# 1/rms of fourteen norms moved from ScalarE's square root to a bit-level seed and three Newton steps on VectorE

## The chip, the cores and the metric

The program runs on one core of a Trainium2 chip. A core has five engines with a queue each: TensorE (PE; its weight loads are shown apart as PEld), VectorE (DVE), ScalarE (ACT), GpSimd (POOL) and SyncE (SP, which here issues nearly all DMAs). Every engine works its own queue in order, and engines wait for each other through semaphores. The metric is the time of one execution in microseconds of the device; lower is better.

## The reference, cut to what matters

One inference step of a decoder trunk with two layers: 512 prompt tokens and 32 sample tokens (8 sequences of 4) of width 1024. Layer 0 mixes tokens with gated linear attention (GLA), layer 1 with sliding-window attention; both also attend to a memory of 256 tokens. Each layer is a SwiGLU network, the token mix, and a second SwiGLU network, and each of the three starts with an RMS norm. There is one more norm ahead of the shared keys and values, one at the end, one over each head of the GLA output, and one over the memory tokens.

```python
def rmsnorm(x, g):
    xf = x.astype(jnp.float32)
    y = xf * lax.rsqrt(jnp.mean(xf * xf, axis=-1, keepdims=True) + EPS)
    return (y * g.astype(jnp.float32)).astype(x.dtype)

def swiglu_half(x, g, w_gu, w_down):
    h = rmsnorm(x, g)
    gate, up = jnp.split(h @ w_gu, 2, axis=-1)
    return 0.5 * ((jax.nn.silu(gate) * up) @ w_down)
```

In each of two layers: `x += swiglu_half(x)`, `x += [tokmix(rmsnorm(x)); memattn(rmsnorm(x))] @ w_out`, `x += swiglu_half(x)`. All inputs and outputs are float32.

## The kernel before, in words

The tokens lie transposed, 128 features to a tile and eight tiles to the width, in two halves: h0 is 256 prompt tokens and the 32 sample tokens (288 columns), h1 the other 256 prompt tokens. Every product of float32 numbers is made of three products of shorter numbers: each operand is split into a rounded part (on ScalarE, L298) and the remainder (on VectorE, L299). So each tile of weights (128x1024, names ending in r as loaded, h and l as split) costs ScalarE about 1.06 us and VectorE about 1.23 us before TensorE can use it, and each tile of activations has such a pair too. A dense product (L356) is 24 matmuls into one PSUM bank: eight feature tiles by three. Three banks (bank_67, bank_68, bank_69 in the order below) take turns for these products, so a product waits until the values of the one three before have been read out of its bank.

The second half of the width of the hidden layer runs as a Strassen-like pair product of both halves (L342), for which `pair` forms sums and differences on VectorE.

A norm is `rstd` (L394): TensorE adds the squares over the features with a column of ones (L404), VectorE scales the mean and adds EPS (L410, two or three columns of 128 numbers), `rsqrt` (L424) makes 1/rms, VectorE multiplies the identity matrix with it (L414), TensorE spreads the diagonal over all partitions with a matrix of ones (L416), and ScalarE copies that out of PSUM (L421). Then `normed` multiplies the tokens (L438) and splits them (L298, L299). `rsqrt` also serves the norm over the GLA heads (L860, twelve columns, named ov).

ScalarE evaluates its functions from tables that hold one set of functions at a time. [...] Where the next function is not in the present set, an instruction ACT_TABLE_LOAD stands ahead of it in ScalarE's queue and bears the line of that function.

Names of norms used below, in order of time: mix_0 is the norm ahead of layer 0's token mix, for h0 at 355 us and for h1 at 543 us; the one for keys and values of h0 at 1066 us; mix_1 for h0 at 1478 us and for h1 at 1630 us; the norms ahead of the two pair products of the second networks at 802 and 1799 us; the final norm of h1 at 2138 us, after which nothing is left but the output. Around mix_0 h0, the keys' norm and mix_1 h0 the same piece of code runs: the norm of h0 is made while TensorE multiplies the last third of the first network for h1 (products g0, u0, g1, u1, g2, u2: gate and up; `late` or `first` in `layer` and `run`).

The order of the instructions within an engine's queue is not that of the code. It is chosen when the kernel is built, by a scheduler that places each instruction by priorities (`high_priority`) and by its own estimate of when it could start, and that also chooses which free weight buffer a load goes to. So a changed instruction list can move others that the code does not touch.

Of the kernel before, what the change touches and what calls it, by code (L numbers as in the profile page):

```python
# [11 lines left out]
F32 = mybir.dt.float32  # L12
F32R = mybir.dt.float32r
U8 = mybir.dt.uint8
AF = mybir.ActivationFunctionType
ALU = mybir.AluOpType
AX = mybir.AxisListType
# [215 lines left out]
class Build:  # L233
# [61 lines left out]
    def split_into(self, h, l, src, scale=None):  # L295
        nc = self.nc
        if scale is None:
            nc.scalar.activation(h, src, AF.Copy)  # L298
            nc.vector.tensor_tensor(out=l, in0=src, in1=h.bitcast(F32), op=ALU.subtract)  # L299
        else:  # L300
            nc.scalar.activation(h, src, AF.Copy, scale=scale)
            nc.vector.scalar_tensor_tensor(out=l, in0=src, scalar=scale, in1=h.bitcast(F32),
# [57 lines left out]
    def copy(self, out, ps, scale=1.0):  # L360
        with self.tc.high_priority(offset=self.AHEAD):
            self.nc.scalar.activation(out, ps, AF.Copy, scale=scale)
        return out
# [6 lines left out]
    def stats(self, x, h):  # L370
# [3 lines left out]
        if self.seen[h] in (1, KD):  # L374
            sq = self.u(n)
            nc.scalar.activation(sq, x, AF.Square)
            self.acc[h].append(sq)
        else:
            sq = self.sqs.u(n)
            nc.scalar.activation(sq, x, AF.Square)  # L380
            nc.vector.tensor_tensor(out=self.acc[h][0], in0=self.acc[h][0], in1=sq, op=ALU.add)
# [12 lines left out]
    def rstd(self, h, banks=None, keep=True):  # L394
# [25 lines left out]
        r = self.u(n)  # L420
        nc.scalar.activation(r, pr[:, :n], AF.Copy)  # L421
        return r

    def rsqrt(self, v, s, t):  # L424
        nc = self.nc
        nc.scalar.activation(s, v, AF.Sqrt)
        nc.vector.reciprocal(t, s)
        nc.vector.scalar_tensor_tensor(out=s, in0=t, scalar=-0.5, in1=t, op0=ALU.mult, op1=ALU.mult)
        nc.vector.tensor_tensor(out=s, in0=s, in1=v, op=ALU.mult)
        nc.vector.scalar_tensor_tensor(out=t, in0=s, scalar=1.5, in1=t, op0=ALU.add, op1=ALU.mult)  # L430

    def normed(self, h, norm, r):
        nc = self.nc
# [919 lines left out]
    def run(self):  # L1353
        nc, d = self.nc, self.d
# [6 lines left out]
        self.mr = None  # L1361
        self.vt, self.state = [None] * 5, [None] * GH
        self.x = [[], []]
        self.layer_ = 0
        with self.tc.high_priority(offset=self.FIRST):
            self.gains = self.const("gains")
            nc.scalar.activation(self.small("set", 1), self.one, AF.Sqrt)
# [31 lines left out]
        nc.vector.tensor_scalar(out=self.gout, in0=self.gout, scalar1=0.5, scalar2=None, op0=ALU.mult)  # L1399
        self.masks = self.cp.tile([P, 9, P], U8, tag="masks", name="masks")  # L1400
        for j in range(3):
            t = self.ld("mask", [P, 3, P])
# [7 lines left out]
        for o, i in (("o_kc", "ckr"), ("o_vc", "cvr")):  # L1410
            nc.sync.dma_start(d[o], d[i][:, 4 * 192:])

        rest = self.layer(0, self.in_a, self.attend_a, d["a_out"], xs)
        r = self.rstd(0)
        xk = self.normed(0, "kv", r)
# [90 lines left out]
```

## Time and profile before

| what | value |
|---|---|
| three timed runs | 2155.02, 2154.74, 2149.47 us; median 2154.74 |
| the profiled execution | 2148.32 us, of which 2146.5 us from the first to the last instruction |
| TensorE busy | 2065.4 us, 96% of the span |
| VectorE busy | 1539.5 us, 72%, 3234 instructions |
| ScalarE busy | 1067.2 us, 50%, 2089 instructions |
| mean granted clock of TensorE | 0.983 of full speed |

The busy shares are means over stages with different limits; what a change in one place is worth is read from who waits there. The time outside the span (1.8 us) is the same kind of start and end for every execution. The granted clock is 1 at 2.4 GHz and 0.5 at 1.2 GHz.

### The profile page before, as it was taken

The numbers are of one execution on the slowest core, as the hardware profiler recorded it, in microseconds if no ns is written. First come the engines' busy times: TensorE is split into PE (matmuls) and PEld (weight loads), VectorE is DVE, ScalarE is ACT, GpSimd is POOL, SyncE is SP. The second block draws the span as 40 slices with busy tenths as digits, with TensorE's granted clock in tenths as the row PEclk, the third lists the DMA queues.
The fourth block names the chain that finished last, engine by engine and source line by source line (L and its number), as shares of the span: only waits on it lengthen the run. The fifth ranks groups of instructions, "written<-read, shape, count | busy, mean of one in ns | idle before, by whom it ended". The sixth has DMA issues, their size and how long they took to land.

```text
span 2146.5 us, 41032 instructions
## 1 busy us (share of the span) xinstructions
PE 2065.4 (96%) x16428; PEld 2000.7 (93%) x16428; DVE 1539.5 (72%) x3234; ACT 1067.2 (50%) x2089; POOL 35.8 (2%) x69
## 2 busy tenths in 40 slices
PE   6999999999999998999999999999998999999998
PEld 6999999998799998999999999999986988999998
DVE  7876675576668869757587776665877877966655
ACT  5554444754646645535355553444544544544434
POOL 5000000000000000000000000000000000000000
PEclk9999999999999999999999999999998999999999
DMA  7533253434454342323354523243443434232344
GB/s 230 157 115 109 79 156 118 138 120 148 152 160 159 125 143 79 108 87 103 113 178 142 177 89 114 74 148 122 151 147 105 143 109 128 89 109 79 110 149 128
DMA packets 90496, 273.03 MB, mean 127 GB/s; under 512 B 11408, under 2 KB 25248, under 8 KB 90272
## 3 DMA queue, kind: packets, MB, share of 16 engines
q1 hardware_dynamic: 89728, 269.87, 39.8%
q8 instruction: 129, 2.11, 0.4%
q14 instruction: 63, 0.52, 0.1%
q10 hardware_dynamic: 576, 0.52, 0.1%
HBM read 264.04 MB, written 7.70 MB: 127 GB/s over the span
## 4 chain that ended last, share of the span: by engine, by line
PE 85%; DVE 8%; DMA 4%; ACT 2%; issue 2%; SPq 0%; DVEq 0%; ACTq 0%
PE bank L356 55%; PE bank L342 21%; PE bank L904 1%; PE bank L1142 1%; DVE u L299 1%; PE bank L1134 1%; DMA u19r<-gu_ffn 0%; PE bank L649 0%; DMA u21r<-gu_ffn 0%; DMA u20r<-gu_ffn 0%; PE bank L705 0%; PE bank L416 0%; PE bank L679 0%; PE bank L1030 0%; PE bank L668 0%
## 5 line engine op out<-in xcount | busy, mean ns | idle before, releaser
L298 ACT ACTIVATE u<-u 128x272 fp32r<-128x272 f32 (+3 forms) x328 | 134.0, 422 | 132.5 <-DVE u L537 55.2
L545 DVE SCALAR_TENSOR_TENSOR x<-bank,x 128x16 f32<-128x16 f32 (+2 forms) x192 | 59.7, 342 | 115.0 <-PE bank L356 114.2
L299 DVE TENSOR_TENSOR u<-u,u 128x272 fp32r<-128x272 f32 (+3 forms) x328 | 137.2, 429 | 3.0 <-ACT u L298 1.2
L356 PE MATMUL bank<-u,d0h 128*128 128x272 f32 (+2 forms) x352 | 71.3, 289 | 0.0
L356 PE MATMUL bank<-u,d1h 128*128 128x272 f32 (+2 forms) x352 | 70.3, 288 | 0.0
L356 PE MATMUL bank<-u,d2h 128*128 128x272 f32 (+2 forms) x352 | 68.6, 289 | 0.4 <-DVE x L755 0.4
L356 PE MATMUL bank<-u,d3h 128*128 128x272 f32 (+2 forms) x352 | 68.0, 290 | 0.0
L356 PE MATMUL bank<-u,d4h 128*128 128x272 f32 (+2 forms) x352 | 67.5, 289 | 0.0
L356 PE MATMUL bank<-u,d5h 128*128 128x272 f32 (+2 forms) x352 | 67.3, 289 | 0.0
L356 PE MATMUL bank<-u,d6h 128*128 128x272 f32 (+2 forms) x352 | 67.1, 288 | 0.0
L356 PE MATMUL bank<-u,d7h 128*128 128x272 f32 (+2 forms) x352 | 67.0, 288 | 0.0
L534 ACT ACTIVATE u<-u 128x272 f32<-128x272 f32 x56 | 24.1, 430 | 73.2 <-DVE u L533 73.2
L356 PEld LDWEIGHTS bank<-u,d0h 128*128 128x128 f32 x352 | 56.3, 188 | 0.2
L356 PEld LDWEIGHTS bank<-u,d2h 128*128 128x128 f32 x352 | 55.4, 188 | 0.9 <-issue 0.5
L356 PEld LDWEIGHTS bank<-u,d1h 128*128 128x128 f32 x352 | 56.1, 188 | 0.0
L356 PEld LDWEIGHTS bank<-u,d3h 128*128 128x128 f32 x352 | 55.3, 188 | 0.3 <-DVE x L580 0.3
L356 PEld LDWEIGHTS bank<-u,d4h 128*128 128x128 f32 x352 | 55.4, 188 | 0.0
L356 PEld LDWEIGHTS bank<-u,d5h 128*128 128x128 f32 x352 | 55.2, 188 | 0.1
L356 PEld LDWEIGHTS bank<-u,d6h 128*128 128x128 f32 x352 | 55.2, 188 | 0.0
L356 PEld LDWEIGHTS bank<-u,d7h 128*128 128x128 f32 x352 | 55.1, 188 | 0.1
L356 PE MATMUL bank<-u,d2l 128*128 128x272 f32 (+2 forms) x176 | 51.0, 290 | 0.0
L356 PE MATMUL bank<-u,d4l 128*128 128x272 f32 (+2 forms) x176 | 50.9, 289 | 0.0
(1178 smaller groups left out, 7664.7 us busy)
## 6 DMA issues: line engine op xcount, KB each, us to landing
g0r<-gu_ffn SPq DMA_DIRECT2D x8, 512.0 KB, 3.5
u0r<-gu_ffn SPq DMA_DIRECT2D x8, 512.0 KB, 3.4
g1r<-gu_ffn SPq DMA_DIRECT2D x8, 512.0 KB, 3.4
u1r<-gu_ffn SPq DMA_DIRECT2D x8, 512.0 KB, 3.5
g2r<-gu_ffn SPq DMA_DIRECT2D x8, 512.0 KB, 3.4
u2r<-gu_ffn SPq DMA_DIRECT2D x8, 512.0 KB, 3.9
g3r<-gu_ffn SPq DMA_DIRECT2D x8, 512.0 KB, 3.5
u3r<-gu_ffn SPq DMA_DIRECT2D x8, 512.0 KB, 3.6
```

Of the source, the lines that this page charges most:

```text
L298: nc.scalar.activation(h, src, AF.Copy)
L299: nc.vector.tensor_tensor(out=l, in0=src, in1=h.bitcast(F32), op=ALU.subtract)
L342: self.nc.tensor.matmul(ps, a[:, k, :], x, start=start and k == 0 and j == 0, stop=k == len(xs) - 1 and j == 2, skip_group_check=True)
L356: self.nc.tensor.matmul(ps, w[:, k, :], x, start=i == 0 and j == 0, stop=i == kc - 1 and j == 2)
L534: nc.scalar.activation(c2, c2, AF.Silu)
L545: nc.vector.scalar_tensor_tensor(out=x, in0=p, scalar=0.5, in1=x, op0=ALU.mult, op1=ALU.add)
L904: nc.tensor.matmul(pv[:, c * half:(c + 1) * half], lhs[:, c * P:(c + 1) * P], second(rhs[:, c * P:(c + 1) * P]), start=True, stop=True)
L1134: nc.tensor.matmul(ps[:, e, P * (1 - back):][:, :P], q[j][64 * half:64 * half + 64, cols], self.keys(kv, half, n - back), start=True, stop ...
L1142: nc.tensor.matmul(dst, self.vt[n - i][:, 64 * kv:64 * kv + 64], pt[i].rearrange("p g t -> p (g t)"), start=i == 0, stop=i == last)
```

## The change

In the first three norms of the run (`bare`: tokens h0, memory, tokens h1) nothing changes. In the fourteen that follow, the square root on ScalarE and the reciprocal on VectorE are replaced by one VectorE instruction that reads the number's bits as an integer, multiplies by -0.5 and adds 0x5f3759df, which gives a rough 1/sqrt; and the three instructions of the Newton step run three times instead of once. All instructions work on 128x2 or 128x3 numbers (128x12 for the GLA heads).

```diff
     def rsqrt(self, v, s, t):
-        nc = self.nc
-        nc.scalar.activation(s, v, AF.Sqrt)
-        nc.vector.reciprocal(t, s)
-        nc.vector.scalar_tensor_tensor(out=s, in0=t, scalar=-0.5, in1=t, op0=ALU.mult, op1=ALU.mult)
-        nc.vector.tensor_tensor(out=s, in0=s, in1=v, op=ALU.mult)
-        nc.vector.scalar_tensor_tensor(out=t, in0=s, scalar=1.5, in1=t, op0=ALU.add, op1=ALU.mult)
+
+        nc = self.nc
+        if self.bare:
+            nc.scalar.activation(s, v, AF.Sqrt)
+            nc.vector.reciprocal(t, s)
+        else:
+            nc.vector.tensor_scalar(out=t.bitcast(I32), in0=v.bitcast(I32), scalar1=-0.5, scalar2=float(0x5f3759df),
+                                    op0=ALU.mult, op1=ALU.add)
+        for _ in range(1 if self.bare else 3):
+            nc.vector.scalar_tensor_tensor(out=s, in0=t, scalar=-0.5, in1=t, op0=ALU.mult, op1=ALU.mult)
+            nc.vector.tensor_tensor(out=s, in0=s, in1=v, op=ALU.mult)
+            nc.vector.scalar_tensor_tensor(out=t, in0=s, scalar=1.5, in1=t, op0=ALU.add, op1=ALU.mult)
...
-        self.layer_ = 0
+        self.layer_, self.bare = 0, True
...
+        self.bare = False
         rest = self.layer(0, self.in_a, self.attend_a, d["a_out"], xs)
```

With the square roots, table loads leave ScalarE's queue: 28 stand in it before, 12 after. And the scheduler places other instructions anew around the norms and, between them, in the two attention stages. In the changed kernel the lines below `rsqrt` have numbers 7 to 9 higher (L564 is L571, L1033 is L1040), those above 1 higher (L298 is L299); its bit instruction is L432 and its Newton step L435 to L437.

First ScalarE's queue at mix_0 h0. L426 is the square root, L564 the tanh of a gate product in the bank named, L298 a split, L421 the copy of the norm. Before (the row that follows the last one is the tanh of bank_67):

```order
L426 ACT_TABLE_LOAD
L426 ACTIVATE r<-r 128x3
L298 ACTIVATE u2h<-u2r 128x1024
L298 ACTIVATE u_4244<-u_4210 128x256
L421 ACTIVATE u_4130<-bank_67 128x288
L298 ACTIVATE agh<-agr 128x1024
L298 ACTIVATE u_4134<-u_4132 128x288
L298 ACTIVATE u_4140<-u_4138 128x288
L298 ACTIVATE u_4146<-u_4144 128x288
L298 ACTIVATE u_4152<-u_4150 128x288
L298 ACTIVATE a_kh<-a_kr 128x1024
L564 ACT_TABLE_LOAD
```

Now:

```order
L571 ACTIVATE u_4215<-bank_68 128x256
L299 ACTIVATE u2h<-u2r 128x1024
L299 ACTIVATE u_4249<-u_4215 128x256
L299 ACTIVATE agh<-agr 128x1024
L422 ACTIVATE u_4135<-bank_67 128x288
L299 ACTIVATE u_4139<-u_4137 128x288
L299 ACTIVATE a_kh<-a_kr 128x1024
L299 ACTIVATE u_4145<-u_4143 128x288
L571 ACTIVATE u_4351<-bank_69 128x256
L299 ACTIVATE u_4151<-u_4149 128x288
L299 ACTIVATE a_qh<-a_qr 128x1024
L571 ACTIVATE u_4283<-bank_67 128x256
```

Both loads and the square root are gone; the tanh of bank_69 stands ahead of that of bank_67, and a second weight split (a_qh) now stands ahead of the latter. On VectorE the remainder of a_q stands ahead of L572 (L565 before) on bank_67 in the same way.

TensorE's queue at the same place: g1 and g2 are gate products, u2 an up product into bank_67, a_k the first product of the token mix. Before:

```order
L356 MATMUL bank_67<-u_810,g1h 128x256
L356 MATMUL bank_67<-u_811,g1h 128x256
L356 MATMUL bank_67<-u_810,g1l 128x256
L356 MATMUL bank_69<-u_804,g2l 128x256
L356 MATMUL bank_69<-u_810,g2h 128x256
L356 MATMUL bank_69<-u_811,g2h 128x256
L356 MATMUL bank_69<-u_810,g2l 128x256
L356 MATMUL bank_67<-u_756,u2h 128x256
```

Now:

```order
L357 MATMUL bank_67<-u_810,g1l 128x256
L357 MATMUL bank_69<-u_4139,a_kh 128x288
L357 MATMUL bank_69<-u_4140,a_kh 128x288
L357 MATMUL bank_69<-u_4139,a_kl 128x288
L357 MATMUL bank_69<-u_4145,a_kh 128x288
L357 MATMUL bank_69<-u_4146,a_kh 128x288
L357 MATMUL bank_69<-u_4145,a_kl 128x288
L357 MATMUL bank_69<-u_4151,a_kh 128x288
L357 MATMUL bank_69<-u_4152,a_kh 128x288
L357 MATMUL bank_69<-u_4151,a_kl 128x288
L357 MATMUL bank_69<-u_4157,a_kh 128x288
L357 MATMUL bank_67<-u_756,u2h 128x256
```

All of g2 now stands ahead of g1, and ten matmuls of the token mix stand between g1 and u2. At the keys' norm (1066 us) it is a whole product, the 24 matmuls of u3, that stands between g1 and u2; at mix_1 h0 ten matmuls of bq0.

VectorE's queue at mix_0 h1, in the GLA stage: L1033 updates states, L717 and L728 belong to the attention of the sample tokens to the memory. Before:

```order
L410 TENSOR_SCALAR r<-bank_68 128x2
L427 RECIPROCAL r<-r 128x2
L712 TENSOR_REDUCE smx<-bank_74 128x1
L428 SCALAR_TENSOR_TENSOR r<-r 128x2
L713 TENSOR_SCALAR smx<-smx 128x1
L429 TENSOR_TENSOR r<-r 128x2
L430 SCALAR_TENSOR_TENSOR r<-r 128x2
L414 TENSOR_SCALAR u_6364<-c_ident,r 128x128 x2
```

Now, from the seventh row after L411 (the L410 of before); between the two stand the bit instruction, the first Newton step and two small steps of the memory attention:

```order
L435 SCALAR_TENSOR_TENSOR r<-r 128x2
L436 TENSOR_TENSOR r<-r 128x2
L723 RECIPROCAL ssm<-ssm 128x1
L437 SCALAR_TENSOR_TENSOR r<-r 128x2
L1040 SCALAR_TENSOR_TENSOR st<-st,ebl,bank_70 96x192 x2
L724 TENSOR_SCALAR u_6757<-u_6757,ssm 128x256
L435 SCALAR_TENSOR_TENSOR r<-r 128x2
L1040 SCALAR_TENSOR_TENSOR st<-st,ebl,bank_72 96x192 x2
L436 TENSOR_TENSOR r<-r 128x2
L735 TENSOR_TENSOR u_6951<-bank_73,c_bm 128x256
L735 TENSOR_TENSOR u_6969<-bank_73,c_bm 128x256
L735 TENSOR_TENSOR u_7126<-bank_73,c_bm 128x256
```

The last Newton instruction and the diagonal (L415) follow behind these rows: four state updates and four instructions of the memory attention that stood behind the diagonal now stand ahead of it.

## Rows read from the trace of the kernel before

**Rows 1.** The page's busy times: engine, busy us, share, instructions.

```profile
PE 2065.4 (96%) x16428; PEld 2000.7 (93%) x16428; DVE 1539.5 (72%) x3234; ACT 1067.2 (50%) x2089; POOL 35.8 (2%) x69
```

**Rows 2.** Waits of TensorE: us in total, times, longest us.

```profile
PE bank L356 <- DVE u L565: 9.7, 4, 2.7
```

**Rows 3.** Groups of ScalarE: count, busy us, mean ns, idle before.

```profile
L426 ACT ACT_TABLE_LOAD x12 | 15.4, 1283 | 0.3
```

**Rows 4.** Line 428, a Newton instruction: count, ns min/median/max, first and last start.

```profile
L428 DVE SCALAR_TENSOR_TENSOR r<-r x15: 140/161/453, 23.6 to 2138.4; 128x2 f32<-128x2 f32 x8, 128x3 f32<-128x3 f32 x7
```

**Rows 5.** Timeline of ScalarE at mix_0 h0: start us, us, instruction, [idle before].

```profile
367.39 1.06 ACT L298 ACTIVATE a_kh<-a_kr 128x1024 fp32r<-128x1024 f32 x1 [0.77 <-PE bank L356]
368.47 1.28 ACT L564 ACT_TABLE_LOAD   x1
369.76 0.38 ACT L564 ACTIVATE u<-bank 128x256 f32<-128x256 f32 x1
```

**Rows 6.** Timeline of VectorE and TensorE at the same place.

```profile
367.67 0.28 PE L356 MATMUL bank<-u,g2l 128*128 128x256 f32 x1
...
368.48 1.23 DVE L299 TENSOR_TENSOR a_kl<-a_kr,a_kh 128x1024 fp32r<-128x1024 f32 x1 [0.51 <-ACT a_kh L298]
...
370.18 0.42 DVE L565 SCALAR_TENSOR_TENSOR u<-u,bank 128x256 f32<-128x256 f32 x1 [0.47 <-ACT u L564]
...
370.66 0.60 PE L356 MATMUL bank<-u,u2h 128*128 128x256 f32 x2 [2.71 <-DVE u L565]
```

**Rows 7.** Timeline of TensorE, keys' norm and mix_1 h0.

```profile
1081.83 0.51 PE L356 MATMUL bank<-u,u2h 128*128 128x256 f32 x2 [2.71 <-DVE u L565]
...
1493.33 0.51 PE L356 MATMUL bank<-u,u2h 128*128 128x256 f32 x2 [2.71 <-DVE u L565]
```

**Rows 8.** Windows: stretch, length, busy us (instructions) by engine, granted clock, DMA.

```profile
370.92:374.32 3.40, 3.40 (x18) 3.40 (x18) 3.19 (x7) 1.63 (x6) 0.00 (x0) 0.50 0.65 204
374.33:377.73 3.40, 3.40 (x28) 3.40 (x28) 3.10 (x7) 2.05 (x4) 0.32 (x1) 1.00 0.22 88
...
1082.10:1085.50 3.40, 3.40 (x31) 3.40 (x31) 3.20 (x7) 1.63 (x6) 0.00 (x0) 1.00 0.67 208
...
1493.90:1497.30 3.40, 3.40 (x18) 3.40 (x17) 3.40 (x8) 1.64 (x5) 0.00 (x0) 0.50 0.65 228
```

**Rows 9.** Timeline of VectorE and TensorE at mix_0 h1.

```profile
544.77 0.48 DVE L414 TENSOR_SCALAR u<-c_ident,r 128x128 f32<-128x128 f32 x2
...
546.17 0.73 DVE L1033 SCALAR_TENSOR_TENSOR st<-st,ebl,bank 96x192 f32<-96x192 f32 x2 [0.34 <-PE bank L1030]
...
547.44 0.71 PE L416 MATMUL bank<-u,ones 128*128 128x128 f32 x4
...
548.40 1.09 DVE L728 TENSOR_TENSOR u<-bank,c_bm 128x256 f32<-128x256 f32 x3 [0.57 <-PE bank L720]
...
555.42 0.43 PE L733 MATMUL bank<-mvc,u 128*32 128x64 f32 x16 [1.30 <-DVE u L438]
```

**Rows 10.** Timeline of VectorE and TensorE at mix_1 h1.

```profile
1632.16 0.17 DVE L427 RECIPROCAL r<-r 128x2 f32<-128x2 f32 x1 [1.02 <-ACT r L426]
...
1632.89 0.65 PE L733 MATMUL bank<-mvc,u 128*32 128x64 f32 x16 [1.67 <-DVE r L428]
```

**Rows 11.** Timeline of VectorE and TensorE at the final norm of h1.

```profile
2137.55 0.16 DVE L410 TENSOR_SCALAR r<-bank 128x2 f32<-128x2 f32 x1 [1.37 <-PE bank L404]
2138.18 0.17 DVE L427 RECIPROCAL r<-r 128x2 f32<-128x2 f32 x1 [0.47 <-ACT r L426]
...
2138.97 0.48 DVE L414 TENSOR_SCALAR u<-c_ident,r 128x128 f32<-128x128 f32 x2
...
2139.31 1.22 PE L416 MATMUL bank<-u,ones 128*128 128x128 f32 x4 [1.79 <-DVE u L414]
```

**Rows 12.** Timeline of VectorE and ScalarE ahead of layer 1's pair product.

```profile
1800.42 0.48 DVE L414 TENSOR_SCALAR u<-c_ident,r 128x128 f32<-128x128 f32 x2
...
1804.28 0.36 ACT L421 ACTIVATE u<-bank 128x256 f32<-128x256 f32 x1
```

More of the change, by code (lines that the diff above doesn't have):

```diff
@@ L14 @@
 U8 = mybir.dt.uint8
+I32 = mybir.dt.int32
 AF = mybir.ActivationFunctionType
```

## The prediction

> **What bounds the kernel now.** Read the page's busy times first [rows 1]: TensorE works for 2065.4 of the span's 2146.5 us, so every other engine matters only where TensorE waits for it, and all such waits together are about 80 us. The waits of TensorE come next [rows 2]. VectorE's line L565 (the up product times its gate) holds up TensorE four times for 9.7 us in all, the longest 2.7 us. Then ScalarE's groups [rows 3], in which a table load takes 1.283 us, and the Newton instruction by itself [rows 4]: 0.161 us as a median. Last, by timeline, every place at which a norm stands, since an average over fifteen norms tells nothing of any one of them.
>
> At mix_0 h0 the chain can be read row by row [rows 5, 6]. ScalarE ends the split of a_k at 368.45, loads the table for tanh until 369.75, makes the tanh until 370.14; VectorE's L565 follows until 370.60 and reads the bank that u2 needs, and u2 starts at 370.66. TensorE's last g2 matmul ended at 367.95: 2.71 us of waiting, of which 1.28 us is the load. The same 2.71 us stands at the keys' norm and at mix_1 h0 [rows 7]. Behind the first and the third the granted clock is 0.50 for a stretch of 3.40 us, in which 18 matmuls ran where 28 run in the next; behind the second it stayed at 1.00, with 31 matmuls [rows 8]. So the lower level costs 10 x 0.121 us (3.40 us / 28) = 1.2 us each of two times, and the wait alone does not decide whether it comes.
>
> **The change part by part.** Per norm ScalarE loses a square root and VectorE a reciprocal; VectorE gains the bit instruction and six Newton instructions, net six. 14 norms x 6 = 84 instructions by 0.161 us [rows 4] is 13.5 us of VectorE, which is busy 72% [rows 1]. Sixteen table loads go (28 to 12): 16 x 1.283 = 20.5 us of ScalarE [rows 3], and 14 square roots of some 0.2 us, 23 us together. I cost both at nothing by themselves: ScalarE is idle half the time [rows 1], and its freed time counts only where TensorE waits behind it. What the path sees of a norm is a chain of small VectorE instructions that each wait for the one before. Its step can be read at the final norm [rows 11]: from L427's start at 2138.18 to L414's at 2138.97 there are four, so 0.198 us each, and from L410 to L414 it took 1.42 us with the square root in it. The new chain is L410, the bit instruction and nine Newton steps, 11 x 0.198 = 2.18 us. A bare norm chain is 0.76 us later, not earlier. That is the sign that goes against the change.
>
> Place by place:
>
> Mix_0 h0. Ten matmuls of the token mix now stand between g1 and u2: 10 x 0.121 = 1.2 us of the 2.71 are filled, if their tiles are ready. The load's 1.28 us no longer stand ahead of bank_67's tanh, but the split of a_q, 1.06 us, does, and on VectorE its remainder, 1.23 us, stands ahead of the product [rows 5, 6]. So u2's start hardly comes earlier, 0.1 to 0.4 us later by my reading of the two queues. I take -0.9; the bounds are 0 (the ten wait too) and -2.71 (the wait goes whole).
>
> Keys' norm. A whole product of 24 matmuls stands there now, 24 x 0.121 = 2.9 us, more than the wait [rows 7, 8]. I take -2.4, since the start of such a product has a few tenths of its own; bounds 0 and -2.71.
>
> Mix_1 h0. Ten matmuls of bq0, as at mix_0 h0: -0.9; bounds 0 and -2.71.
>
> The two stretches at the lower clock [rows 8] cost 2.4 us. A shorter wait may or may not bring them back, and the keys' norm shows a full wait without one. I take half, -1.2; bounds 0 and -2.4, or +1.2 if the keys' norm gets one.
>
> Mix_0 h1 [rows 9]. Here VectorE's own order is against it. Ahead of the diagonal L414 there now stand four state updates (0.73 x 2 = 1.46 us), three L728 (1.09 us), one more instruction of that width (some 0.36 us by L728's mean) and six more small steps (6 x 0.198 = 1.19 us): 4.1 us together. The diagonal ended at 545.25 and its matmul L416 stood at 547.44, so 2.2 us are covered, by GLA matmuls that keep TensorE busy. 4.1 - 2.2 = 1.9 us could show; the instructions moved ahead have their own consumers, which now come earlier, and a wait of 1.30 us for a normed tile further on may change as well. I take +1.5; bounds -1.3 and +4.1.
>
> Mix_1 h1 [rows 10]. VectorE sat idle for 1.02 us for the square root, and TensorE waited 1.67 us for the instruction after it, L428. That idle time goes, but VectorE's queue is longer by six steps, 1.2 us, of which some stand ahead of what TensorE waits for. I take -1.0; bounds -1.67 and +0.2 (1.2 less 1.02).
>
> Final norm of h1 [rows 11]. Nothing lies beside it: TensorE waits 1.79 us for L414. +0.76 whole; bounds 0 (the steps run closer) and +1.2 (six steps on top, the square root having cost nothing).
>
> The two norms ahead of the pair products [rows 12]. L414 ended at 1800.90 and the copy out of PSUM began at 1804.28, so over 3 us of matmuls lie between, and 0.76 us more are hidden. I take +0.3 for both; bounds 0 and 2.4 (two times six steps).
>
> The other seven norms are made during products of 24 matmuls (2.9 us), which cover 0.76 us: 0. Without that cover each costs up to 1.2 us.
>
> Sum: -0.9 - 2.4 - 0.9 - 1.2 + 1.5 - 1.0 + 0.76 + 0.3 = -3.8 us on the profiled execution of 2148.32, so 2144.5. This execution is 6.4 us below the median of the timed runs and below each of them, while the three themselves differ by 5.6. I therefore put the sum on the mean of all four, 2151.9: 2148.
>
> A rule of the Trainium skill speaks for a larger gain. In rows 5 the split ends at 368.45, the load begins at 368.47 and the tanh follows 0.01 us behind it: 1.28 us and nothing else beside it. The page "ScalarE: Activation LUTs", section "What ACT_TABLE_LOAD costs", gives 1283 ns for the load, which this trace repeats to the nanosecond [rows 3], and about 1380 ns of draining with every switch, 2.66 us together, which it does not show here. By the rule the three sites would give back 3 x 2.66 = 8.0 us in place of my 4.2, and the sum would be -7.6.
>
> **The rivals.**
>
> First, the waits go whole. With both loads off ScalarE's queue all that feeds the three u2 could be early enough. Then 3 x 2.71 = 8.1, the two slow stretches 2.4 and the wait of 1.67 go, against 0.76 at the end: -11.4, 2140.5. For it: the three waits are equal to the hundredth, so one thing causes them, and it is the load that stands in all. Against it: at two sites a weight split takes the load's place.
>
> Second, the change does what it says and nothing comes of it: what is filled at the three sites is waited for one product later, since the splits of weights on ScalarE and VectorE, 1.06 and 1.23 us a tile, are still as many. Net 0, give or take 2: 2152. For it: VectorE is 3.10 to 3.40 us busy in stretches of 3.40 right behind each wait [rows 8], so it is the engine behind schedule there, and the change gives it more work. Against it: the loads stand on ScalarE, which was the releaser of VectorE's 0.47 us idle time [rows 6].
>
> Third, slower. VectorE's in-order queue is the mechanism. Each chain has six more steps, between which the new order puts other work, so the diagonal and L416 come late. Price: 1.9 to 4.1 at mix_0 h1, about the same six steps and more (2.5) at mix_1 h1, 1.2 at each pair, 0.76 at the end, against gains of 4.2 at the three sites at most: +3 to +7, about 2157. It decides from the point at which the diagonal is later than the 2.2 us of cover [rows 9]. Against it: the new order also moved TensorE's L416 back behind more matmuls.
>
> That it doesn't do what it says: the number of steps is fixed and no branch depends on values, so the rough seed cannot change the time; the loads are gone from the queue. I give this no chance of its own.
>
> **How the numbers follow.** The forecast has 0.46, the first rival 0.24, the second 0.16, the third 0.14. What a measurement of this kernel can tell from no change is about 0.3%, 6.4 us. The forecast lies inside of it at its centre; I count a third of it (0.15) as faster, 0.02 as slower and 0.29 as the same. The first rival is faster but for 0.02, the second is the same but for 0.02 faster and 0.01 slower, and the third splits into 0.09 slower and 0.05 the same. Together: faster 0.39, same 0.49, slower 0.12. The range goes from the first rival, 2140, to the third, 2157; what is left out is the unknown costs of all places falling on one side. The forecast's own range is 2144 to 2152.
>
> **What would show it right or wrong.** In the profile of the changed kernel the waits of TensorE behind the product of u2 (now L572) should read about 1.5 us at mix_0 h0 and mix_1 h0 and near 0 at the keys' norm; if all are 0, the first rival holds, if the same microseconds stand one product later, the second. The granted clock behind the first and the third shows whether the stretches at 0.50 went. At mix_0 h1 the distance from the diagonal to L416 and the wait ahead of the latter decide the third. At the end L410 to L414 (L411 to L415 now) should read 2.2 us. I am wrong if TensorE waits anew in the attention stages, where the order moved most and where I have counted single places only, or if the whole kernel's clock differs from 0.983.

## The result and the profile after

| | before | changed |
|---|---|---|
| median of 14 runs each, us | 2154.04 | 2159.97 |
| lowest to highest | 2145.40 to 2157.97 | 2156.64 to 2167.38 |
| profiled execution, us | 2148.32 | 2156.77 |
| ratio to before, with 95% interval | 1 | 1.0035 [1.0024, 1.0046] |

The changed kernel is slower by 0.35%. The forecast was 2148 us, inside of 0.3%; the range 2140 to 2157 does not hold 2159.97. The third rival had the sign, and named two of the places at which time was lost; its mechanism holds in part (E7, E9 and E10 below).

The page of the changed kernel, first part, answering to [rows 1] (engine, busy us, share, instructions):

```profile
PE 2075.3 (96%) x16428; PEld 2003.9 (93%) x16428; DVE 1547.6 (72%) x3318; ACT 1041.7 (48%) x2059; POOL 34.8 (2%) x69
```

VectorE has the 84 instructions more and is 8.1 us busier (13.5 were worked out), ScalarE 25.5 us less busy (23). Neither figure explains the result. The one that does is TensorE's: it runs as many matmuls as before and is busy 9.9 us longer, of a span that is 8.5 us longer. So taken over the whole kernel the loss is not waiting but slower multiplying. The waits for L572 (L565 before), which the change was to shorten, did fall (us in all, times, longest), from the 9.7 us of [rows 2]:

```profile
PE bank L357 <- DVE u L572: 3.9, 6, 1.5
```

To place the loss, the time from the start of one named matmul to the start of another is taken in each trace, the same two in all. Nearly all of it lies in three stretches; the three sites of [rows 6, 7], called lead sites here, gain. The columns E1 to E10 are the experiments below, one profile each; all but the first column are differences to it in us.

| stretch of before, us | length | changed | E1 | E2 | E3 | E4 | E5 | E6 | E7 | E8 | E9 | E10 |
|---|---|---|---|---|---|---|---|---|---|---|---|---|
| 351-400, mix_0 h0 | 48.89 | -2.60 | -0.55 | -2.11 | -2.67 | +0.03 | -2.61 | -2.09 | +0.03 | +0.06 | +0.03 | -2.62 |
| 536-616, mix_0 h1, GLA | 79.97 | +5.81 | +1.21 | +9.10 | +7.43 | -0.31 | +1.92 | +10.52 | +5.24 | +2.99 | +1.28 | +7.85 |
| 660-798, second GLA stage | 137.65 | +6.48 | -0.11 | +7.78 | +6.44 | +4.21 | -0.06 | +0.04 | -0.01 | 0.00 | +0.01 | +7.76 |
| 1062-1100, keys' norm h0 | 37.77 | -2.48 | -0.54 | -1.92 | -2.47 | +1.57 | -2.49 | -0.59 | +0.03 | -2.49 | +1.54 | -2.48 |
| 1474-1510, mix_1 h0 | 36.17 | -2.66 | -0.59 | -2.13 | -2.63 | -0.10 | -2.66 | -0.55 | 0.00 | -2.67 | -0.03 | -2.64 |
| 1604-1674, mix_1 h1 | 70.67 | +6.42 | -1.69 | +6.18 | +6.92 | +0.87 | +0.07 | +0.05 | -1.62 | -1.54 | +4.31 | +3.55 |
| 1793-1870 | 76.69 | -1.69 | -0.14 | -1.72 | -1.70 | -0.39 | -1.69 | -0.06 | -0.36 | +0.35 | -1.11 | -1.73 |
| 2080-2139, final norm h1 | 58.81 | +0.74 | +0.75 | -0.01 | -0.43 | 0.00 | -0.01 | +0.76 | +0.01 | +0.01 | +0.01 | +0.73 |

How far single profiles of one order scatter can be read down the table: with the order of before the second stretch runs from -0.3 to +3.0 (E1, E4, E5, E8, E9), the sixth from -1.7 to +0.9, the third only from -0.1 to 0. The fourth reads +1.6 in E4 and +1.5 in E9, where 3.4 us behind the wait ran at half clock, which before did not. With the order of the changed kernel (E2, E3, E6 and E10 too) the second stretch runs from +5.8 to +10.5, so in two of three stretches a single figure is good to a few us only. The stretches left out sum to -1.6 for the changed kernel.

**The lead sites** gained more than was forecast. TensorE at mix_0 h0 in the changed kernel (start us, us, instruction, [idle before]):

```profile
368.83 0.53 PE L357 MATMUL bank<-u,a_kh 128*128 128x288 f32 x2 [0.19 <-DVE u L572]
...
371.53 0.50 PE L357 MATMUL bank<-u,u2h 128*128 128x256 f32 x2 [0.85 <-DVE u L572]
```

The ten products of the token mix fill the wait, and 0.85 of 2.71 us is left, with 0.19 ahead of the ten; u2 itself starts 0.2 us later relative to the stretch's start, as worked out. Behind it the windows (stretch, length, busy us of PE, PEld, DVE, ACT, POOL with instructions, granted clock, DMA) show that the stretches at half clock of [rows 8] went at both sites:

```profile
371.60:375.00 3.40, 3.40 (x28) 3.40 (x29) 3.40 (x10) 1.68 (x4) 0.00 (x0) 1.00 0.48 154
...
1498.70:1502.10 3.40, 3.40 (x28) 3.40 (x29) 3.40 (x10) 1.65 (x4) 0.00 (x0) 1.00 0.46 159
```

**Mix_0 h1.** VectorE in the changed kernel, from the scaled mean to the diagonal:

```profile
542.51 0.16 DVE L411 TENSOR_SCALAR r<-bank 128x2 f32<-128x2 f32 x1 [2.27 <-PE bank L405]
...
544.30 0.14 DVE L437 SCALAR_TENSOR_TENSOR r<-r 128x2 f32<-128x2 f32 x1
545.31 0.73 DVE L1040 SCALAR_TENSOR_TENSOR st<-st,ebl,bank 96x192 f32<-96x192 f32 x2 [0.87 <-PE bank L1037]
545.97 0.34 DVE L724 TENSOR_SCALAR u<-u,ssm 128x256 f32<-128x256 f32 x1
...
547.29 1.09 DVE L735 TENSOR_TENSOR u<-bank,c_bm 128x256 f32<-128x256 f32 x3 [0.19 <-PE bank L727]
548.29 0.15 DVE L437 SCALAR_TENSOR_TENSOR r<-r 128x2 f32<-128x2 f32 x1
548.48 0.48 DVE L415 TENSOR_SCALAR u<-c_ident,r 128x128 f32<-128x128 f32 x2
```

From the mean to the diagonal it takes 5.97 us. Before, the starts of the two chains, at mix_0 h1 and mix_1 h1, stood at

```profile
543.36 0.16 DVE L410 TENSOR_SCALAR r<-bank 128x2 f32<-128x2 f32 x1 [2.27 <-PE bank L404]
...
1630.13 0.15 DVE L410 TENSOR_SCALAR r<-bank 128x2 f32<-128x2 f32 x1
...
1633.80 0.48 DVE L414 TENSOR_SCALAR u<-c_ident,r 128x128 f32<-128x128 f32 x2
```

and the diagonal of the first at 544.77 [rows 9]: 1.41 us, so it is 4.6 us longer now, near the 4.1 worked out. Part of it is that a Newton step stands behind L1040, which waits 0.87 us for TensorE. What was not worked out is what follows on TensorE. Before, two rows of 14 dense products of the token mix stand at 550.39 (with a wait of 0.35 us in it) and at 558.22:

```profile
550.39 0.85 PE L356 MATMUL bank<-u,agh 128*128 128x256 f32 x2 [0.39 <-ACT u L298]
...
558.22 0.39 PE L356 MATMUL bank<-u,agh 128*128 128x256 f32 x1
```

In the changed kernel:

```profile
549.92 1.22 PE L417 MATMUL bank<-u,ones 128*128 128x128 f32 x4
...
556.11 0.66 PE L740 MATMUL bank<-mvc,u 128*32 128x64 f32 x16 [1.12 <-DMA mvc<-mv]
...
565.93 0.67 PE L357 MATMUL bank<-u,agl 128*128 128x256 f32 x1
```

The first long row of dense products (17 matmuls) starts at 565.93. Until then TensorE has mostly small matmuls (192 columns of the states and 64 of the memory attention) with single dense ones between them, and from 546.6 on the granted clock is 0.50. The same window in before and after, and the windows of the two other stretches, TensorE's clock in the column behind POOL; first before:

```profile
540.00:570.00 30.00, 26.30 (x291) 19.95 (x290) 20.45 (x59) 14.29 (x41) 0.00 (x0) 0.94 0.51 158
672.00:710.00 38.00, 36.54 (x302) 35.77 (x302) 35.62 (x115) 24.91 (x63) 1.43 (x7) 1.00 0.49 157
1600.00:1650.00 50.00, 38.56 (x362) 28.48 (x362) 30.38 (x122) 17.25 (x62) 0.00 (x0) 0.76 0.25 78
```

and the changed kernel:

```profile
540.00:570.00 30.00, 27.60 (x244) 18.59 (x243) 17.61 (x61) 7.72 (x30) 0.00 (x0) 0.66 0.49 141
672.00:710.00 38.00, 33.87 (x273) 32.84 (x272) 34.74 (x111) 23.75 (x64) 1.36 (x7) 0.96 0.42 136
1600.00:1650.00 50.00, 36.51 (x321) 25.02 (x321) 28.06 (x117) 13.36 (x61) 0.00 (x0) 0.62 0.27 81
```

Read microsecond by microsecond, the clock (1 is 2.4 GHz, 0.50 is 1.2 GHz) was at 0.50 from 558.6 to 562 before, and from 546.6 to 567.1 in the changed kernel: 20 us instead of 3. (The profile of before is at the low end: with its order on TensorE the clock was at 0.50 for 3 us in E4 and for 10 to 14 us in E1, E5, E8 and E9; with the new order, E2, E3, E6 and E10 included, for 20 to 31 us.) From 540 to 570 us TensorE is busy longer and does 47 matmuls less.

**Mix_1 h1.** VectorE and TensorE of the changed kernel:

```profile
1635.25 0.15 DVE L411 TENSOR_SCALAR r<-bank 128x2 f32<-128x2 f32 x1
...
1638.50 0.42 DVE L1183 TENSOR_TENSOR u<-bank,u 128x256 f32<-128x256 f32 x1 [2.31 <-PE bank L1179]
1638.84 0.15 DVE L437 SCALAR_TENSOR_TENSOR r<-r 128x2 f32<-128x2 f32 x1
...
1641.76 0.48 DVE L415 TENSOR_SCALAR u<-c_ident,r 128x128 f32<-128x128 f32 x2
...
1642.68 1.22 PE L417 MATMUL bank<-u,ones 128*128 128x128 f32 x4
1645.47 0.58 PE L357 MATMUL bank<-u,bq0h 128*128 128x256 f32 x1 [1.56 <-ACT u L299]
```

The square root's idle time went, but a Newton step now stands behind L1183, which waits 2.31 us for TensorE; 6.51 us from the mean to the diagonal instead of 3.67. L417 stands last of the small matmuls, so nothing covers the norm behind it: 1.56 us of waiting, at half clock.

**The second GLA stage.** Before, a product of 21 matmuls (mm12) stood on TensorE between mm11 and the first L904 (L911 now). In the changed kernel L911 comes right behind mm11 and waits for ScalarE, and L675 waits further on. First the wait of before, then the two:

```profile
678.45 0.51 PE L356 MATMUL bank<-u,mm12h 128*128 128x256 f32 x2 [1.13 <-DVE u L839]
```

```profile
684.50 0.63 PE L911 MATMUL bank<-u 96*128 96x64 f32 x4 [1.70 <-ACT u L935]
...
697.73 0.63 PE L675 MATMUL bank<-c_ident,u 128*128 128x128 f32 x4 [1.61 <-DVE u L669]
```

Of the 6.5 us, 3.2 are idle time of TensorE (3.0 before, 6.1 now), about 2 are longer dense products (busy 115.9 and 118.0 us; 3.4 us of the stretch, behind the wait at L911, are at half clock), and 0.9 are six L417 of the norm at 650 us, which stand ahead of this stretch before.

**The end** went as worked out: L411 to L415 took 2.16 us (2.18 forecast), and TensorE's wait before L417 grew from the 1.79 us of [rows 11] by 0.75:

```profile
2145.23 0.16 DVE L411 TENSOR_SCALAR r<-bank 128x2 f32<-128x2 f32 x1 [1.37 <-PE bank L405]
...
2147.39 0.48 DVE L415 TENSOR_SCALAR u<-c_ident,r 128x128 f32<-128x128 f32 x2
...
2147.73 1.23 PE L417 MATMUL bank<-u,ones 128*128 128x128 f32 x4 [2.54 <-DVE u L415]
```

### The profile page after: what moved, and what is told of

Read it like the earlier page. It is cut to its first block, busy times and chain, and to the rows that moved or that the text cites. A ratio compares the mean times of both kernels' runs of the same rounds, so it can differ in the third digit from the quotient of the medians.

```text
span 2155.0 us, 41084 instructions
## 1 busy us (share of the span) xinstructions
PE 2075.3 (96%) x16428; PEld 2003.9 (93%) x16428; DVE 1547.6 (72%) x3318; ACT 1041.7 (48%) x2059; POOL 34.8 (2%) x69
## 3 DMA queue, kind: packets, MB, share of 16 engines
q8 instruction: 129, 2.11, 0.4%
## 4 chain that ended last, share of the span: by engine, by line
PE 83%; DVE 9%; DMA 3%; ACT 2%; issue 2%; SPq 0%; DVEq 0%; ACTq 0%
PE bank L357 52%; PE bank L343 22%; PE bank L911 1%; DVE u L300 1%; PE bank L1149 1%; PE bank L405 1%; PE bank L1141 1%; PE bank L712 0%; PE bank L656 0%; DMA u20r<-gu_ffn 0%; DMA u19r<-gu_ffn 0%; PE bank L417 0%; DMA u18r<-gu_ffn 0%; PE bank L1037 0%; PE bank L686 0%
## 5 line engine op out<-in xcount | busy, mean ns | idle before, releaser
L299 ACT ACTIVATE u<-u 128x272 fp32r<-128x272 f32 (+3 forms) x328 | 132.9, 420 | 112.9 <-DVE u L544 51.4
```

## The experiments

The change does two things: it makes the norms' chains longer on VectorE, and it makes the scheduler place many hundred instructions differently. **Theory O** is that the new order costs the time, **theory S** that the six steps per norm do. They are told apart by giving one kernel's arithmetic the other's order. For that a function at the end of `run` ties each instruction to the one that stands ahead of it on its engine in the other build (an edge of order alone, no wait):

```python
for e in queues:                       # PE, DVE, ACT, SP, POOL
    for a, b in zip(row[e], row[e][1:]):   # row: e's instructions as the other build has them
        tc.add_manual_dep(b, a.name, NoSync)
```

Of a norm's small instructions only the last keeps a place given so; the others, and a square root that the other build lacks, are left to the scheduler. Edits below are to `rsqrt` or to `row`.

**E1, new arithmetic in the old order.**

```diff
 # the changed kernel
+row = queues of the kernel before
```

> The changed kernel's arithmetic (bit instruction and nine Newton instructions in all fourteen norms, no square root, 12 table loads) with every engine's queue pinned to the order of the kernel before; only the norms' own small instructions differ. Theory O (the order that the scheduler chose costs the time): the three attention stages (540 to 615, 655 to 775 and 1600 to 1650 us) take as long as before, give or take 1.5 us each; the three waits for u2 fall from 2.71 us by the load's 1.28 to about 1.4; 0.76 more at the end; in all -3 us, about 2150, ratio 0.997 to 1.000. Theory S (the six added steps per norm on VectorE cost the time): the stages are late as in the changed kernel, +12 or more of its +18 us, and the whole is 2160 or more, ratio 1.003 or more.

Measured: 2151.90 us, ratio 0.9998 [0.9985, 1.0011]. The second GLA stage and mix_1 h1 take no longer than before, and the stretch of mix_0 h1 is inside of its scatter; 84 more instructions on VectorE cost nothing that can be measured. But the gain of 3 us did not come either: the stretches of the lead sites are only 0.55 us shorter. TensorE's waits and, below, ScalarE and VectorE in E1 (L373 is the dense product, L625 is L572, L624 the tanh, L315 the split, L316 the remainder):

```profile
PE bank L373 <- DVE u L625: 8.0, 4, 2.2
```

```profile
368.22 1.06 ACT L315 ACTIVATE a_kh<-a_kr 128x1024 fp32r<-128x1024 f32 x1 [0.76 <-PE bank L373]
369.18 0.36 ACT L624 ACTIVATE u<-bank 128x256 f32<-128x256 f32 x1
369.44 1.05 ACT L315 ACTIVATE a_qh<-a_qr 128x1024 fp32r<-128x1024 f32 x1
...
369.31 1.23 DVE L316 TENSOR_TENSOR a_kl<-a_kr,a_kh 128x1024 fp32r<-128x1024 f32 x1 [0.50 <-ACT a_kh L315]
```

The load is gone and the tanh comes at once, and each wait for u2 is still 2.15 us: the next thing, on VectorE, is the remainder of a_k (1.23 us), ahead of L625. So in the old order the loads are worth 0.56 us a site; the rest of the 2.6 us gained in the changed kernel comes with the new order, which puts products into the wait, and at mix_0 h0 and mix_1 h0 with the full clock behind it. By the rule of the Trainium skill ("ScalarE: Activation LUTs", "What ACT_TABLE_LOAD costs"), a load and a drain of 1380 ns with every switch, the three sites would have given back 8.0 us; they give 1.7. This run alone does not tell the drain from the load, since not even the load's 1.28 us comes back where the remainder of a_k is next in line. That no drain stands beside the load is read from [rows 5].

**E2, old arithmetic in the new order.**

```diff
 # the kernel before
+row = queues of the changed kernel
```

> The arithmetic of the kernel before (square root on ScalarE, reciprocal, one Newton step in all norms) with every engine's queue pinned to the order of the changed kernel. Theory O: the attention stages are late as in the changed kernel, +12 to +18 us there, and the gain at the three waits for u2 stays at least in part: 2157 to 2166, ratio 1.002 to 1.006. Theory S: six steps fewer in each norm, so the stages are as before and the whole is 2147 to 2154, ratio 1.000 or less.

Measured: 2164.68 us, ratio 1.0060 [1.0042, 1.0078]. As theory O has it, and theory S falls: with one Newton step and the square root in every norm the three stretches are +9.1, +7.8 and +6.2 us, and the lead sites gain 2 us each with the loads in the queue, to which the loads' removal adds 0.5 us, as it did in E1.

**E3, one Newton step in the new order.**

```diff
-for _ in range(1 if self.bare else 3):
+for _ in range(1):
+row = queues of the changed kernel
```

> The changed kernel in its own order, pinned, with one Newton step in place of three in the fourteen norms (two steps are left out, so 1/rms is rough): as many VectorE instructions as before, no square roots, no table loads. Theory O: like the changed kernel but for about 1.2 us at the end and at most 1 us elsewhere: 2156 to 2160, ratio 1.001 to 1.003. Theory S: the loss of the attention stages goes and the gains at the three waits stay: 2142 to 2148, ratio 0.995 to 0.998.

Measured: 2160.40 us, ratio 1.0037 [1.0022, 1.0051], a little above what was expected; the changed kernel has 1.0035. Two steps less in fourteen norms are worth 1.2 us at the end (+0.74 to -0.43) and nothing that can be told elsewhere.

**E4, one norm changed, at 650 us.**

```diff
-if self.bare:
+if nth_norm != 6:   # h0, ahead of layer 0's second network
```

> Only one norm is changed, the one of h0 ahead of layer 0's second network, at 650 us, queues as the scheduler sets them: in this build they differ from before between 655 and 770 us and a little at 800 and 1500 us. Theory O: the stretch from 655 to 775 us is some 5 us longer, as in the changed kernel, though no other norm is changed: 2156 to 2160, ratio 1.001 to 1.004. Theory S: at most one chain of 0.76 to 1.2 us is added, hidden behind a product or not: ratio 0.9995 to 1.0008.

Measured: 2154.42 us, ratio 1.0016 [1.0004, 1.0028]. One chain, which waits for nobody new, makes the stretch from 660 to 798 us 4.2 us longer. The row of the wait at L911 (L914 here) is the same as in the changed kernel:

```profile
680.54 0.63 PE L914 MATMUL bank<-u 96*128 96x64 f32 x4 [1.70 <-ACT u L938]
```

In this build some 340 of TensorE's matmuls between 660 and 800 us (and some 70 behind) stand elsewhere than before, and the loss came with them. Six steps in one norm were enough to trigger it.

**E5, the new order without its three bad stretches.**

```diff
 # the changed kernel
-if self.bare:
+if self.bare or final norm of h1:
+row = queues of the changed kernel; of the kernel before in 536-616, 655-800 and 1600-1690 us
```

> The changed kernel's arithmetic, with square root kept in a fourth norm, the last one (h1 at the end). Queues pinned: in the order of the changed kernel everywhere but in three stretches (536 to 616, 655 to 800 and 1600 to 1690 us), where they are pinned in the order of the kernel before. Theory O: the gains of the changed kernel stay (2.6 at mix_0 h0, 2.5 and 1.6 at the keys' norms, 2.7 at mix_1 h0, about 1 behind 1758) and its losses in the three stretches and at the end go: 2142 to 2146, ratio 0.995 to 0.9975. Rival (the gains ahead of a stretch are given back in it, since its own waits, on transfers and on the softmax chains, set its end): 2150 or more, ratio 0.9985 or more.

In the traces the queues of this run have the order of before from 536 to 880 us, not only to 800.

Measured: 2142.89 us, ratio 0.9955 [0.9942, 0.9969]. The gains are not given back: this is faster than both kernels, by 10 us than the one before. The profile is the slowest of its six executions.

**E6, only the GLA stage in the new order.**

```diff
 # as E1
+row = queues of the kernel before; of the changed kernel in 536-616 us
```

> As the run with the changed arithmetic in the order of the kernel before, but one stretch, 536 to 616 us (GLA of h0 with the memory attention, the norm mix_0 h1 in it), is pinned in the order of the changed kernel. Theory O with the clock as the means: this stretch alone is +5 to +8 us, with a granted clock of 0.50 for 15 us or more in it, and everything else stays: 2156 to 2160, ratio 1.002 to 1.004. Rival (the loss needs the orders of other stages too, such as earlier transfers): +2 us or less, ratio 1.0005 or less.

Measured: 2158.73 us, ratio 1.0032 [1.0021, 1.0043], against 0.9998 for E1. One stretch, alone, costs as much as the whole change does net. Its clock, beside 0.83 of E1 in the same window:

```profile
540.00:570.00 30.00, 27.37 (x225) 17.00 (x222) 17.39 (x59) 6.68 (x24) 0.00 (x0) 0.57 0.50 141
```

**E7, only the diagonal late.** VectorE's and TensorE's rows at mix_0 h1 in the order of before, but:

```diff
 # the kernel before, pinned
-L430, L414, then L1033 x4, L717, L728 x3 and one small step
+L1033 x4, L717, L728 x3 and one small step, then L430, L414
-L416, then L720, L1030 x8, L733 (the first half)
+L720, L1030 x8, L733 (the first half), then L416
```

> The arithmetic of the kernel before, every queue pinned in its order, but for one thing: at mix_0 h1 the diagonal and the last Newton instruction stand behind the nine VectorE instructions that the changed kernel has ahead of them, and the two matmuls L416 behind the nineteen matmuls (states and memory attention). The dense products of the token mix keep their places. If the late diagonal is the cause of the loss at 536 to 616 us: +3 to +6 us in that stretch with the clock at 0.50 for 15 us or more, ratio 1.001 to 1.003. If the late places of the dense products (moved behind all of the memory attention) are the cause: +0 to +2 us, ratio 1.000 to 1.001.

Measured: 2155.28 us, ratio 1.0010 [1.0002, 1.0019]; in the profile the stretch is 5.24 us longer and the clock is at 0.50 from 546.2 to 566.7. TensorE in E7 (L433 is L416, L793 is L733):

```profile
552.33 1.23 PE L433 MATMUL bank<-u,ones 128*128 128x128 f32 x4
...
555.00 1.04 PE L373 MATMUL bank<-u,agh 128*128 128x256 f32 x2 [0.65 <-ACT u L315]
...
563.71 0.65 PE L793 MATMUL bank<-mvc,u 128*32 128x64 f32 x16 [2.23 <-DMA mvc<-mv]
...
564.29 0.58 PE L373 MATMUL bank<-u,agh 128*128 128x256 f32 x1
```

The dense products kept their places and still came 4.6 us (first row) and 6.1 us (second row) later, since they need the norm and stand behind small matmuls, one of which waits 2.23 us for a transfer. So the late diagonal by itself costs something, but the timed loss, 2.2 us, is less than the profile's, and far less than the 7 us or so by which E6 stands above E1. The time alone lies where both expectations meet; what speaks for the first is the stretch in the profile, beyond the +3.0 of the old order.

**E8, three norms changed.**

```diff
-if self.bare:
+if nth_norm not in (9, 10, 11):   # keys h0, keys h1, mix_1 h0
```

> Only three norms changed, queues as the scheduler sets them: the keys' norms of h0 and h1 (1066 and 1145 us) and mix_1 h0 (1478 us). In this build the orders of the three attention stages stay nearly those of the kernel before. Theory O: the gains of these three places alone, 2.5 + 1.6 + 2.7 = 6.8 us: 2145 to 2148, ratio 0.9965 to 0.998. Rival: given back in the stage at 1600 us, ratio 0.999 or more.

Measured: 2145.33 us, ratio 0.9967 [0.9956, 0.9978]. No order is pinned. The two sites of h0 gain 2.5 and 2.7 us as in the changed kernel, and the stages stay in their order.

**E9, only the norm mix_1 h1 late.**

```diff
 # the kernel before
+row = queues of the kernel before; of the changed kernel for some 25 instructions
+      a queue on PE, DVE and ACT around mix_1 h1
```

> The arithmetic of the kernel before, every queue pinned in its order but for some 25 instructions a queue around the norm mix_1 h1 (1625 to 1645 us), which stand in the order of the changed kernel: VectorE's chain of the norm has the softmax's products with its wait for TensorE ahead of its last steps, and L416 stands behind the eight products of the values, with nothing left behind it but the dense products that need it. If the late diagonal causes the loss at 1600 to 1675 us: +4 to +7 us in that stretch, ratio 1.002 to 1.003. If the earlier half of the new order there (transfers, scores) causes it: +0 to +2 us, ratio 1.001 or less.

Measured: 2159.82 us, ratio 1.0037 [1.0024, 1.0051], more than expected; 4.31 us in the stretch of the profile (whose execution, 2153.87 us, is the fastest of the five: the others lose more than the profile shows). TensorE in E9 waits as in the changed kernel, to the hundredth:

```profile
1643.86 1.23 PE L433 MATMUL bank<-u,ones 128*128 128x128 f32 x4
1646.65 0.38 PE L373 MATMUL bank<-u,bq0h 128*128 128x256 f32 x1 [1.56 <-ACT u L315]
```

**E10, the diagonal early in the new order.** The opposite of E7:

```diff
 # the changed kernel, pinned
+L437 (last), L415 ahead of L1040 x4, L724, L735 x3
+L417 ahead of L727, L1037 x8, L740
```

> The changed kernel in its own order, pinned, but at mix_0 h1 the last Newton instruction and the diagonal stand ahead of the nine VectorE instructions, and L417 ahead of the nineteen matmuls, as in the kernel before. The dense products of the token mix stay where the changed kernel has them, behind the memory attention. If the late diagonal alone causes the loss at 536 to 616 us: -4 us or more there, ratio to before 1.000 to 1.002. If the late places of the dense products keep TensorE at small matmuls whatever the diagonal does: -1.5 us or less there, the clock at 0.50 for 15 us or more, ratio 1.003 to 1.004.

Measured: 2162.90 us, ratio 1.0047 [1.0035, 1.0060], above both expectations; nothing comes back. The diagonal's matmul stands at 547.58, as early as before, and the clock is 0.50 from 545.2 to 569.1. The dense products, which the new order has behind the memory attention, start their first long row at 567.87:

```profile
567.87 0.67 PE L373 MATMUL bank<-u,agl 128*128 128x256 f32 x1
```

So E7 and E10 together: a late diagonal holds up the dense products where they stand early, and the order that the scheduler made around the late diagonal has them late anyway. In the profiles either keeps the clock at 0.50 until 566 us or later. In the changed kernel it is the places of the dense products that count: with the diagonal early the loss stays.

## Why the prediction was wrong

- **Sites of the three waits.** The direction was right and the size too small: -0.9, -2.4, -0.9 and -1.2 for the clock, 5.4 together; measured 2.60 + 2.48 + 2.66 = 7.7. The fill by ten products and by u3 was as worked out; of the two stretches at 0.50 the forecast counted half, and both went, in every profile with the new order there (the first also in E6, with the old one). The first rival, with 10.5 for these places, was as far off on the other side, and its reason fails: E1 shows that without the new order the loads' removal leaves 2.15 of each 2.71 us.
- **Mix_0 h1, +1.5, is the step that failed most**, with mix_1 h1. The diagonal came 4.6 us later (4.1 worked out), but its price was set as what 2.2 us of cover leave over, and TensorE's own order had no term. That order has the dense products behind the memory attention: their first long row starts at 565.93, where rows stood at 550.39 and 558.22, the clock is at 0.50 for 20 us instead of 3, and the stretch is 5.8 us longer (5.8 to 10.5 in the five profiles with the new order). The bound of +4.1 did not hold it, because it took TensorE's rate as given. E10 shows that this needs no late diagonal; a late diagonal without it (E7) lost 2.2 us.
- **Mix_1 h1, -1.0** should have been +6.4. The square root's idle 1.02 us did go; the order put a step behind an instruction that waits 2.31 us, and its place was in the queue to be read, though not the wait. E9 shows that this neighbourhood alone costs as much as the whole change does net; which of the instructions moved in it do so was not separated.
- **"The other seven norms: 0"** (there are six beside the eight that it prices) was right of their chains and wrong of what the change does there: +6.5 from 660 to 798 us, where no chain waits. E4 shows it with one norm changed, E1 and E5 that it goes with the old order. The diff of the orders showed hundreds of moved instructions in this stage; the sum had no term for them. One of the prediction's signs of being wrong, TensorE waiting anew in the attention stages, came true here (3.2 us) and at mix_1 h1 (11.2 us of idle time before, 13.6 now), but not at mix_0 h1.
- **The end, +0.76, and the two norms ahead of the pairs** came near the forecast: +0.74, and no wait at the latter (+0.3 forecast for both).
- **Freed ScalarE and longer VectorE at nothing**: right; E1 and E3 bear it out from both sides.
- **The third rival** named VectorE's in-order queue and the cover of 2.2 us as the point from which it decides. The places at mix_0 h1 and mix_1 h1 hold (E6, E9); of the mechanism, the late diagonal, E7 shows that it costs 2.2 us by itself, and E10 that the loss at mix_0 h1 does not need it. That its price, +3 to +7, holds the 6 us measured is partly luck, since both of its sides were too small: gains of 9.4 with the stretch behind 1793, losses of 19.4, a third of them from 660 to 798 us, which it did not name, while the pairs that it priced at 1.2 each cost nothing. It was given a chance of 0.14, because each place was priced as a single wait.

Not settled: which of the moved instructions between 660 and 798 us makes the loss there. The gain of 1.7 us behind 1793 goes with the new order (E2, E3, E5 and E10 have it, E1 and E6 do not); its cause was not sought.

## What to carry to other kernels

Where a scheduler sets the order at build time, a change has two parts: what its instructions cost, and what order they bring about, everywhere. The second can be the larger by far, so run the new arithmetic in the old order and the old arithmetic in the new before explaining anything by the instructions. A chain of tiny dependent steps is an invitation to put long or waiting instructions between them on an in-order engine: read in the new queue what stands between the first and the last, and above all which of it waits. And price a late norm by the dense work that depends on it, with the clock that TensorE is granted meanwhile, not by the wait that shows in front of it.

## What the runs showed of the hardware

At mix_0 h1 the granted clock decided more than the waits: from 536 to 616 us TensorE's idle time was 5.1 us before and 4.9 in the changed kernel, its busy time 74.8 and 80.9. All twelve profiles show the same matmuls busy for longer, the longer the clock was at 0.50 in this stretch: 74.8 us with 3.4 us at 0.50 (before and E4), 77.4 with 10.2 (E1, E9), 78.5 and 78.8 with 13.7 (E5, E8), 80.9 with 20.5 (E7 and the changed kernel), 81.4 to 82.6 with 23.9 (E2, E3, E10) and 85.4 with 30.7 (E6).

The clock fell to 0.50 between 544 and 548 us, while TensorE ran matmuls of 192 columns and fewer almost without a gap, in all profiles but those of before and E4, also in those with the old order on TensorE (E1, E5, E8, E9). Before and E4 ran the same matmuls there and kept 1.00, so these rows do not tell what decides it. With the old order the clock was back at full by 564 at the latest (E8 has one more short stretch, to 572), with the new one, and in E7, not before 566. In the changed kernel, E2, E3, E6 and E10 it came back within 4 us of the start of the first long row of dense products, and in E1, E5, E8 and E9 2 to 3 us behind theirs; in E7 not behind the first row, at 555.00, but 2.4 us behind the start of the second.

The six small VectorE instructions per norm, 0.2 us each from start to start in a chain, cost 0.75 us where nothing lies beside them, and nothing that E1 could tell (its interval is 0.13% to either side) in the thirteen other norms.
